# A hybrid decoder layer: the input projection by seven products of blocks, and the mLSTM heads as a stage of their own

## The chip, the cores and the metric

The kernel runs on one core of a Trainium2 chip. The core has a matmul engine (PE, whose weight loads, PEld, overlap its products), three engines for other arithmetic (DVE, ACT and POOL) and SP, which issues the DMAs. The metric is the time of one execution in device microseconds, lower is better. It is in float32, and each matmul operand is cut into a high and a low part of a reduced format, so a product of two matrices is three matmuls: low by high, high by low, and high by high.

## The reference

One decoder layer over 1024 tokens of width 1024. What matters here is its first third:

```python
h = rmsnorm(x, ln1[l])
z = h @ w_in[l]
ml_qk, ml_v, ml_o, ml_i, ml_f, fx_q, fx_k, fx_v, fx_f = jnp.split(z, splits, axis=-1)
ml_qk = jax.nn.silu(causal_conv(ml_qk, ml_conv_w[l], ml_conv_b[l]))
mq, mk = jnp.split(ml_qk.astype(jnp.float32), 2, axis=-1)
...
mh = mlstm_chunkwise(mq, mk, mv, ig, lf)
mh = mh * lax.rsqrt(jnp.mean(mh * mh, axis=-1, keepdims=True) + EPS)
...
ml_out = (mh.reshape(B, S, ML_W) * jax.nn.sigmoid(ml_o)).astype(x.dtype)
fx_out = forgetting_attention(fq, fk, fv, flf).reshape(B, S, FX_W)
x = x + jnp.concatenate([ml_out, fx_out], axis=-1) @ w_out[l]
```

There are four mLSTM heads of width 128 (queries and keys pass a causal convolution of four taps and a silu; an output gate `ml_o`) and eight heads of forgetting attention (fx) of width 64. Then follow cross-attention into 256 memory tokens, a squared-ReLU MLP of width 4096, and a final norm.

## The kernel before

Activations lie with the features on the 128 partitions and the tokens along the free dimension, in two halves of 512 tokens. A tile framework orders each engine's instructions and gives out buffers; program order is the priority, and an instruction whose buffer or operand is not there yet can be overtaken. Some stretches are fixed in order by hand (`in_order`). Working buffers have names and small counts: `act` (seven of 128 x 8 x 512), `w4` (five of 128 x 1024), `z4` (two), `wr` for raw weights (two), `wh` and `wl` for their cut parts (three each), and `r_a` to `r_f`, `r_p`, `r_y` of 128 x 512 (one or two each, from `w2`). PSUM has eight banks (`sc` three, `tp` two, `mm`, `m2` (rows name it m) and `ov` one each).

The parts that matter, in program order:

- Lines 381 to 423: x is cut into the operands `h` (high and low for each half, gain folded in), and the first mLSTM values and the gates are made along the way.
- Lines 676 to 682: the other half of the values (`token_major`, eight units of 24 matmuls with 256 columns), the gate rows, and the memory tokens' preparation. All mLSTM values stay in two `act` buffers, `mv`.
- `ml_project` (L656): for each mLSTM head five output tiles of 128 features: the key, an fx query, the query, an fx key, and the output gate. Each tile is eight blocks of the contraction times three matmuls times two halves, by `proj` (L258). `conv_silu` (L502) follows the keys and queries, `carried` and `carry` make the state that the first half of the tokens hands to the second.
- `ml_head` (L568): for each half of the tokens four blocks: scores on PE, weights `exp` on ACT, a mask on POOL, products on DVE, a cut on ACT and DVE, and the sum with the values in the bank `ov`. Then (after its first `yield`) the closing: the factors go through DRAM (`facd`) to a row, and are multiplied in. The numerators of the two halves lie in the two `r_f` buffers until then.
- Line 683 on: head by head, `ml_head` of one head stands ahead of `ml_project` of the next, whose `next(closing)` calls place the steps of the closing between projections.
- Line 1088 on: 13 leading slots of the attention (scores only), then the fx values (`token_major` with `w_fv`, sixteen units), then the attention slots, in which a filler of key and value units of the cross-attention and of output units runs at a given rate.

`mm3` (L184) records every three-matmul product, so its three lines L186 to L188 gather most of PE's time, and `split` (L131) every cut, with ACT at L134 or L137 and DVE at L135 or L138. A sum of the helper `sub` has line L1339.

## Time and profile before

| what | value |
| --- | --- |
| timed runs, median of 3 | 1512.34 us (1508.72 to 1514.9) |
| span of the profiled execution, first to last instruction | 1509.2 us |
| granted PE clock, mean over that span | 0.997 |
| DMA | 303.04 MB, mean 201 GB/s |
| HBM read and written | 202.75 MB and 98.82 MB |

Of the profiled execution the page gives the span and no other time of its own; the median of the timed runs is 3.1 us above that span, and the lowest of them 0.5 us below it. A line of the groups view gives line, engine, operation, the written tile and those read, shapes, count, busy time, the mean of one in ns, and the engine's idle time ahead of the group with what ended it. The windows view gives busy time of each engine in stretches of the span. PE's busy time is modelled from pipelined matmuls: a matmul shown with 395 ns starts 230 ns after the one before it.

### The profile page before, as it was taken

To read this page: it belongs to the slowest core of one execution; us is meant where nothing else is said; L and a number is where in the kernel's file an instruction comes from. 1 tells how busy PE (TensorE), PEld (TensorE's weight loads), DVE (VectorE), ACT (ScalarE), POOL (GpSimd) and SP (SyncE) were. 2 spreads that over 40 slices of the span, in tenths; PEclk is the share of its full clock that TensorE was granted. 3 is DMA by queue.
4 is the path that set the end of the run, shared out by engine and by line. 5 is a ranking of instruction groups with operands and counts; after the bars stand their busy time and mean duration, and the time that the engine had idled before them with its cause. 6 is when DMAs were issued, how large, how long until landed. Compare 5 with 4: busy or idle time off the path is not lost.

```text
span 1509.2 us, 22358 instructions
## 1 busy us (share of the span) xinstructions
PE 1493.0 (99%) x7806; PEld 1263.7 (84%) x7806; DVE 1122.7 (74%) x1803; ACT 757.7 (50%) x1440; POOL 528.7 (35%) x545
## 2 busy tenths in 40 slices
PE   9999999999999999999999999999999999999997
PEld 9988888889899888788988878888888888888887
DVE  7766676664788875667767899989996678787765
ACT  7324343334688764566654467566664521122134
POOL 1003030414365441623300044454544365553312
PEclk9999999999999999999999999999999999999999
DMA  6322333435777877853354447676678677776623
GB/s 243 115 79 95 98 108 126 132 129 153 247 261 256 284 248 246 271 169 126 128 182 159 147 155 279 235 261 248 217 273 292 264 279 279 279 272 251 247 88 112
DMA packets 124276, 303.04 MB, mean 201 GB/s; under 512 B 13810, under 2 KB 28460, under 8 KB 117252
## 3 DMA queue, kind: packets, MB, share of 16 engines
q1 hardware_dynamic: 124164, 301.62, 57.3%
q8 instruction: 61, 1.00, 0.3%
q14 instruction: 51, 0.42, 0.1%
HBM read 202.75 MB, written 98.82 MB: 200 GB/s over the span
## 4 chain that ended last, share of the span: by engine, by line
PE 90%; DMA 4%; DVE 3%; ACT 1%; issue 1%; POOL 1%; POOLq 0%; DVEq 0%; SPq 0%; ACTq 0%
PE tp L186 8%; PE tp L187 8%; PE tp L188 8%; PE sc L186 6%; PE sc L188 6%; PE sc L187 6%; PE mm L186 5%; PE m L188 5%; PE m L186 5%; PE m L187 5%; PE mm L188 5%; PE mm L187 5%; PE ov L801 2%; PE ov L186 2%; PE ov L187 2%; PE ov L188 2%
## 5 line engine op out<-in xcount | busy, mean ns | idle before, releaser
L186 PE MATMUL tp<-act,wl 128*128 128x512 f32 (+1 forms) x440 | 172.6, 392 | 0.0
L187 PE MATMUL tp<-act,wh 128*128 128x512 f32 (+1 forms) x440 | 172.1, 391 | 0.0
L188 PE MATMUL tp<-act,wh 128*128 128x512 f32 (+1 forms) x440 | 171.8, 392 | 0.0
L135 DVE TENSOR_TENSOR wl<-wr,wh 128x1024 fp32r<-128x1024 f32 (+2 forms) x99 | 131.4, 1327 | 27.0 <-ACT wh L134 26.7
L134 ACT ACTIVATE wh<-wr 128x1024 fp32r<-128x1024 f32 (+2 forms) x99 | 99.8, 1008 | 85.7 <-PE tp L188 32.7
L186 PE MATMUL mm<-act,wl 128*128 128x512 f32 (+1 forms) x332 | 124.8, 376 | 2.6 <-DVE r_c L138 2.1
L188 PE MATMUL mm<-act,wh 128*128 128x512 f32 (+1 forms) x332 | 124.1, 374 | 0.0
L187 PE MATMUL mm<-act,wh 128*128 128x512 f32 (+1 forms) x332 | 123.8, 373 | 0.0
L186 PE MATMUL m<-act,wl 128*128 128x512 f32 (+1 forms) x308 | 113.8, 369 | 0.6 <-DVE wl L135 0.6
L188 PE MATMUL m<-act,wh 128*128 128x512 f32 (+1 forms) x308 | 113.8, 369 | 0.0
L187 PE MATMUL m<-act,wh 128*128 128x512 f32 (+1 forms) x308 | 113.7, 369 | 0.0
L188 PE MATMUL sc<-act,wh 128*128 128x512 f32 (+1 forms) x280 | 105.6, 377 | 0.0
L187 PE MATMUL sc<-act,wh 128*128 128x512 f32 (+1 forms) x280 | 105.6, 377 | 0.0
L186 PE MATMUL sc<-act,wl 128*128 128x512 f32 (+1 forms) x280 | 105.6, 377 | 0.0
L1612 POOL TENSOR_TENSOR z<-wr 128x256 f32<-128x256 f32 x56 | 52.9, 966 | 131.8 <-DMA wr<-w_ff2q 126.7
L188 PEld LDWEIGHTS tp<-act,wh 128*128 128x128 f32 x440 | 82.7, 188 | 19.0
L186 PEld LDWEIGHTS tp<-act,wl 128*128 128x128 f32 x440 | 82.7, 188 | 18.5
L187 PEld LDWEIGHTS tp<-act,wh 128*128 128x128 f32 x440 | 82.7, 188 | 18.2
L134 ACT ACTIVATE wh<-z 128x1024 fp32r<-128x1024 f32 (+1 forms) x54 | 55.5, 1027 | 81.8 <-POOL z L1612 62.3
L135 DVE TENSOR_TENSOR wl<-z,wh 128x1024 fp32r<-128x1024 f32 (+1 forms) x54 | 77.7, 1439 | 11.4 <-ACT wh L134 11.4
L134 ACT ACTIVATE w<-wr 128x768 fp32r<-128x768 f32 (+3 forms) x35 | 28.0, 801 | 107.4 <-PE tp L186 33.0
L186 PEld LDWEIGHTS mm<-act,wl 128*128 128x128 f32 x332 | 62.7, 189 | 14.2 <-DVE r_c L138 2.6
(734 smaller groups left out, 4387.2 us busy)
## 6 DMA issues: line engine op xcount, KB each, us to landing
act<-right SPq DMA_DIRECT2D x49, 1024.0 KB
right<-w SPq DMA_DIRECT2D x56, 256.0 KB
wr<-w_ff2q SPq DMA_DIRECT2D x28, 512.0 KB
right<-r_d SPq DMA_DIRECT2D x49, 256.0 KB
right<-r_e SPq DMA_DIRECT2D x49, 256.0 KB
act<-fqk SPq DMA_DIRECT2D x48, 256.0 KB
wr<-w_in SPq DMA_DIRECT2D x20, 512.0 KB
wr<-w_ff SPq DMA_DIRECT2D x20, 512.0 KB
```

The lines of the kernel that those rows point to most:

```text
L134: s.activation(hi, src, AF.Copy)
L135: return v.tensor_tensor(out=lo, in0=src, in1=hi.bitcast(F32), op=ALU.subtract)
L186: nc.tensor.matmul(ps, w[1], x[0], start=first, stop=False, skip_group_check=more)
L187: nc.tensor.matmul(ps, w[0], x[1], start=False, stop=False, skip_group_check=more)
L188: nc.tensor.matmul(ps, w[0], x[0], start=False, stop=last, skip_group_check=more)
L801: nc.tensor.matmul(self.ov[:, c0:], self.fv[:, self.j], t[:, c0:], start=self.j == 0 and t is self.p[1], stop=self.last and t is self.p[0])
L1612: g.tensor_tensor(out=o, in0=x, in1=y, op=op)
```

## The change

The 20 tiles of the input projection are taken as ten pairs of two tiles (two for the gates, then for each head a pair of key and query and a pair of fx query and key). For a pair, the weights are a 2 x 2 arrangement of blocks (two tiles by two halves of the contraction) and h another (two halves of the contraction by two halves of the tokens), and the product is made by seven products of blocks with sums before and after, instead of eight. The sums of h's blocks (t1 to t4) are made by `in_right`, which loads x again; the sums of the weights by `left_in`; the sums after by `InPair.run`. Keys and queries (`kqd`), gates (`ogd`) and mLSTM values (`mvd`) are stored to DRAM. The heads then form a stage of their own, which loads them back (`ml_loads`), with four units of the fx values placed around each head. In the head's loop `carry` stands ahead of the closing of the head before. Half of the key and value units of the cross-attention are taken out of the attention slots and put behind the 13 leading slots, and the filler's rate goes from 4.6 to 3.5.

The diff, cut to its core:

```diff
-    mv = (act(), act())
+    mvd = dram.tile([MLH, P, 8, 2 * P], F32, name="mvd")
     def mv_sink(t, c, ps):
-        o = mv[c][:, t].rearrange("p (h e c) -> p h e c", h=2, e=2)
+        o = rotate("b", "p", "c").bitcast(F32R).rearrange("p (h e c) -> p h e c", h=2, e=2)
         split(o[:, :, 0], o[:, :, 1], ps.rearrange("p (h c) -> p h c", h=2), rcol[:, t : t + 1])
+        load(mvd[2 * c : 2 * c + 2, :, t].rearrange("h p c -> p h c"), o.bitcast(F32).rearrange("p h e c -> p h (e c)"))
...
-    def conv_silu(n, hi, lo):
-        w = weights(a["w_in"][n])
-        z = z4()
-        g.memset(z[:, 0:3], 0.0)
-        for _, hf, ps in proj(w, h, 1):
-            v.tensor_tensor(out=z[:, 3 + hf * TH : 3 + hf * TH + TH], in0=ps, in1=row[:, hf * TH : hf * TH + TH], op=ALU.mult)
-        y = z4()[:, :T]
+    def conv_silu(z, which, hd):
+        n = MLH * which + hd
+        y = w4()
         cw = VEC["conv_w"] + 4 * n
-        v.tensor_scalar(out=y, in0=z[:, 0:T], ...)
+        s.activation(y, z[:, 0:T], AF.Identity, scale=vec[:, cw : cw + 1], bias=...)
         for j in range(1, 4):
             v.scalar_tensor_tensor(out=y, in0=z[:, j : j + T], scalar=vec[:, cw + j : cw + j + 1], in1=y, op0=ALU.mult, op1=ALU.add)
         t = z[:, 0:T]
         s.activation(t, y, AF.Tanh, scale=0.5)
         v.scalar_tensor_tensor(out=y, in0=t, scalar=1.0, in1=y, op0=ALU.add, op1=ALU.mult)
-        split(hi, lo, y, 0.5)
-        return y
+        split(t.bitcast(F32R), y.bitcast(F32R), y, 0.5)
+        load(kqd[hd, which, 0], t)
+        load(kqd[hd, which, 1], y)
+    def whole(parts, hf):
+        t = w2("p")
+        c = slice(hf * TH, hf * TH + TH)
+        g.tensor_tensor(out=t, in0=parts[0][:, c].bitcast(F32), in1=parts[1][:, c].bitcast(F32), op=ALU.add)
+        return t
...
-    def fx_project(which, n):
...
-    def ml_project(hd):
...
+    I_RIGHT = {}
+    for c, hf, k0 in (("11", 0, 0), ("21", 0, 4), ("22", 1, 4)):
+        I_RIGHT[c] = [both(h[hf], lambda t: t[:, k0 + k]) for k in range(4)]
+    for c in ("t1", "t2", "t3"):
+        t = act()
+        I_RIGHT[c] = [(t[:, k], t[:, 4 + k]) for k in range(4)]
+    I_RIGHT["t4"] = [(t[:, :TH], t[:, TH:]) for t in (w4(dt=F32R) for _ in range(4))]
+    def in_right(k):
+        x = {}
+        for c, tag, hf, n in (("11", "d", 0, k), ("12", "e", 1, k), ("22", "f", 1, 4 + k), ("21", "p", 0, 4 + k)):
+            x[c] = w2(tag)
+            load(x[c], a["x"][:, n, hf * TH : hf * TH + TH])
+            s.activation(x[c], x[c], AF.Copy, scale=vec[:, VEC["ln1"] + n :][:, 0:1])
+        y = x["11"]
+        sub(y, x["12"], y)
+        split(*I_RIGHT["t1"][k], y)
+        sub(y, x["22"], y, g)
+        split(*I_RIGHT["t2"][k], y)
+        sub(x["12"], x["22"], x["12"], g)
+        split(*I_RIGHT["t3"][k], x["12"])
+        sub(y, x["21"], y, g)
+        split(*I_RIGHT["t4"][k], y)
+    for k in range(4):
+        in_right(k)
+    I_NAMES = {1: "11", 2: "21", 5: "t1", 6: "t2", 3: "22", 7: "t3", 4: "t4"}
+    i_cycle = ("sc", "mm", "tp", "sc", "m2", "tp", "sc", "ov")
...
+    in_pairs = [("o", 0), ("o", 1)]
+    for hd in range(MLH):
+        in_pairs += [("kq", hd), ("fx", hd)]
...
+    in_both = lambda p_: [(q_, i) for i in I_NAMES for q_ in (p_, p_ + 1)]
+    in_jobs = in_both(0)
+    for p_ in range(2, IP):
+        in_jobs += [(p_, 1)] + ([(p_ - 1, 4)] if p_ > 2 else []) + [(p_, i) for i in (5, 2, 6, 3, 7)]
+    in_jobs.append((IP - 1, 4))
...
+    def left_in(p_, group):
+        if group == 0:
+            in_raws[p_] = [sb("wr", [P, 1024], 2) if p_ != 1 else z4()[:, :1024] for _ in range(2)]
+            for raw, n in zip(in_raws[p_], reversed(in_tiles(*in_pairs[p_]))):
+                load(raw, a["w_in"][n])
+        r2, r1 = in_raws[p_]
+        x11, x12, x21, x22 = r1[:, :TH], r1[:, TH:], r2[:, :TH], r2[:, TH:]
+        if group == 0:
+            h22, l22 = (w2(t, dt=F32R) for t in "bc")
+            split(h22, l22, x22)
...
+        hi, lo = (sb(t, [P, 1024], 3, F32R) for t in ("wh", "wl"))
+        split(hi, lo, (r1, r2, r1)[group])
+        if group == 0:
+            by = g if p_ > 1 else v
+            by.tensor_tensor(out=x21, in0=x21, in1=x22, op=ALU.add)
+            sub(x22, x21, x11, by)
+            sub(x12, x12, x22, by)
+            sub(x11, h22.bitcast(F32), x22, by)
+            by.tensor_tensor(out=x11, in0=x11, in1=l22.bitcast(F32), op=ALU.add)
...
+    class InPair:
...
+        def run(self, i, l):
+            r = I_RIGHT[I_NAMES[i]]
+            at_ = {1: "a", 2: "a", 5: "c", 3: "c", 6: "b", 7: "b", 4: "b"}[i]
+            if i in (1, 5, 6):
+                setattr(self, at_, i_bank())
+            ps = getattr(self, at_)
+            for k in range(4):
+                mm3(ps, both(l, lambda t: t[:, k]), r[k], i in (1, 5, 6) and k == 0, k == 3, True)
+            u = self.u
+            if i == 1:
+                self.p1 = w2("p") if self.kind != "o" else firsts[:, TH * self.i :][:, :TH]
+                s.activation(self.p1, ps, AF.Copy)
+            elif i == 2:
+                v.tensor_tensor(out=self.room("11", "a", "y"), in0=ps, in1=self.row_of("11"), op=ALU.mult)
+                self.done("11")
+            elif i == 5:
+                self.add(self.room("22", "e"), ps, self.p1)
...
+        def scale(self, c):
+            g.tensor_tensor(out=self.u[c], in0=self.u[c], in1=self.row_of(c), op=ALU.mult)
+            self.done(c)
+        def done(self, c):
+            n, hf = int(c[0]) - 1, int(c[1]) - 1
+            x, at_ = self.u[c], slice(hf * TH, hf * TH + TH)
+            if self.kind == "o":
+                s.activation(x, x, AF.Tanh, scale=0.5)
+                load(ogd[2 * self.i + n, :, at_], x)
+            elif self.kind == "fx":
+                hi, lo = w2("d", dt=F32R), x.bitcast(F32R)
+                split(hi, lo, x, None if n else FXD ** -0.5)
+                load(fqk[n, 0, self.i, :, at_], hi.bitcast(F32))
+                load(fqk[n, 1, self.i, :, at_], x)
+            elif c in ("12", "21"):
+                conv_silu(self.z[n], 1 - n, self.i)
+    firsts = w4()
+    for at, (p_, i) in enumerate(in_jobs):
+        while in_prep and in_first[in_prep[0]] <= at + 5:
+            left_in(*in_prep.pop(0))
...
+        pair.run(i, in_cuts.pop((p_, i)))
...
+    def ml_loads(hd):
+        qk = quarters(F32R)
+        for t, src in zip(qk, (kqd[hd, 1, 0], kqd[hd, 1, 1], kqd[hd, 0, 0], kqd[hd, 0, 1])):
+            load(t.bitcast(F32), src)
+        mv = [w4((P, 4, 256), F32R) for _ in range(2)]
+        for i, t in enumerate(mv):
+            load(t.bitcast(F32), mvd[hd, :, 4 * i : 4 * i + 4])
+        og = w4()
+        load(og, ogd[hd])
+        return qk[2:], qk[:2], lambda j: mv[j // 4][:, j % 4], og
...
     for hd in range(MLH):
-        closing = ml_head(hd, *ready)
+        q, k, values, og = ml_loads(hd)
+        weighed = weigh(hd)
+        state = carried(hd, whole(k, 0), values, *weighed)
+        sums = carry(hd, q, whole(q, 1), *state)
+        next(closing, None)
+        fv_next(1)
+        next(closing, None)
+        fv_next(1)
+        closing_now = ml_head(hd, q, k, values, og, *sums)
+        next(closing, None)
+        closing = closing_now
         next(closing)
-        if hd < MLH - 1:
-            ready = ml_project(hd + 1)
+        fv_next(2)
+    fv_next(16)
...
-    units = []
+    units, early = [], []
     for n in range(XH):
+        if n == 2:
+            early, units = units, []
         units += [key_unit(2 * n), value_unit(n), key_unit(2 * n + 1)]
...
-    token_major(a["w_fv"], fv_sink, between={4: lambda: next(closing, None)})
     hm = act().rearrange("p a b -> p (a b)").rearrange("p (e k c) -> p e k c", e=2, k=KT)
     load(hm.bitcast(F32), hmd)
+    for i, (srcs, run) in enumerate(early):
+        if i == 3:
+            next(closing, None)
+        for step in run([weights(src) for src in srcs]):
+            f = step[2] if step[1] else None
+            while f:
+                f = f()
...
-    RATE, DELAY = 4.6, 3
+    RATE, DELAY = 3.5, 3
```

More of the change, by code (lines that the diff above doesn't have):

```diff
@@ L540, in carried @@
             for t in (kl, kh):
-                nc.tensor.matmul(ps[:, 0:256], t[:, j * P : (j + 1) * P], mv_of(hd, j), start=j == 0 and t is kl, stop=j == 3 and t is kh)
+                nc.tensor.matmul(ps[:, 0:256], t[:, j * P : (j + 1) * P], values(j), start=j == 0 and t is kl, stop=j == 3 and t is kh)
         c32 = w2("c", P)
@@ new lines, in hybrid_layer @@
+    in_both = lambda p_: [(q_, i) for i in I_NAMES for q_ in (p_, p_ + 1)]
[3 more added lines that the diff above has]
+    in_jobs.append((IP - 1, 4))
+    I_GROUP = {1: 0, 2: 0, 5: 1, 6: 1, 7: 2, 3: 2}
+    in_first = {}
+    for at, (p_, i) in enumerate(in_jobs):
+        if i in I_GROUP:
+            in_first.setdefault((p_, I_GROUP[i]), at)
+    in_prep = sorted(in_first, key=in_first.get)
@@ new lines, in hybrid_layer, with fv_next @@
+    banks[:] = ["mm", "tp", "m2", "tp"]
+    fv_steps = [t for c in range(2) for t in [token_units(a["w_fv"], fv_sink, c)]]
+    def fv_next(n):
+        while n and fv_steps:
+            try:
+                next(fv_steps[0])
+                n -= 1
+            except StopIteration:
+                fv_steps.pop(0)
+    for hd in range(MLH):
[10 more added lines that the diff above has]
+        closing = closing_now
```

130 lines of the change are left out of this document (76 added, 54 removed).

## The prediction

> **What bounds the kernel now.** I read the page first: the busy table, then the chain that ended last.
>
> ```profile
> span 1509.2 us, 22358 instructions
> ...
> PE 1493.0 (99%) x7806; PEld 1263.7 (84%) x7806; DVE 1122.7 (74%) x1803; ACT 757.7 (50%) x1440; POOL 528.7 (35%) x545
> ...
> PE 90%; DMA 4%; DVE 3%; ACT 1%; issue 1%; POOL 1%; POOLq 0%; DVEq 0%; SPq 0%; ACTq 0%
> ```
>
> The matmul engine (PE) is busy all the time and carries 90% of the chain. As a busy PE need not be a full PE, I next took the windows view, cut where the work around the change begins and ends. Its columns are length, then busy time and instruction count of PE, weight load, DVE, ACT and POOL, then the granted clock, the DMA share and GB/s.
>
> ```profile
> 61.40:331.20 269.80, 269.80 (x1291) 223.31 (x1290) 178.24 (x271) 97.39 (x158) 50.88 (x63) 1.00 0.34 109
> 331.20:393.00 61.80, 60.39 (x486) 59.00 (x485) 34.81 (x86) 27.97 (x68) 22.50 (x28) 1.00 0.58 182
> 393.00:590.00 197.00, 196.01 (x1253) 174.67 (x1252) 158.01 (x413) 145.01 (x397) 97.02 (x149) 1.00 0.76 257
> ...
> 900.00:1000.00 100.00, 100.00 (x430) 80.38 (x429) 90.50 (x101) 67.00 (x107) 47.06 (x30) 1.00 0.74 261
> ```
>
> The rows are the input projection with the mLSTM heads among it; the forgetting values (fv) with the 13 leading slots; the attention slots; and a stretch of the MLP's first product, which already uses seven products. That last row holds only 512-column matmuls and gives a rate: 100/430 = 0.2326 us each. The groups view of 61.4 to 331 by shape counts the same kind here (each row stands for three, L186 to L188, with equal counts):
>
> ```profile
> L186 PE MATMUL tp<-act,wl 128*128 128x512 f32 x160 | 63.6, 398 | 0.0
> ...
> L186 PE MATMUL mm<-act,wl 128*128 128x512 f32 x80 | 31.8, 398 | 0.0
> ...
> L186 PE MATMUL m<-act,wl 128*128 128x512 f32 x80 | 31.6, 395 | 0.0
> ```
>
> 3 x (160 + 80 + 80) = 960 = 20 tiles x 2 halves x 8 x 3. At 0.2326 that is 223.3 of the 269.8 us; 331 small matmuls of the heads share the other 46.5, with no idle time ahead of any group. So the stage is bound by matmul count.
>
> **The change part by part.**
>
> *Seven products.* Ten pairs x 7 products x 4 blocks x 3 = 840 matmuls of 512 columns in place of 960. 120 x 0.2326 = **-27.9 us**. This is arithmetic in the code, so "it doesn't do what it says" is no case here.
>
> *The start.* Blocks t1 to t4 have to be made from x, read a second time, and the first two pairs' weights summed on DVE. What can this hide behind?
>
> ```profile
> 40.00:61.00 21.00, 21.00 (x181) 20.41 (x181) 16.55 (x42) 10.59 (x23) 1.01 (x1) 1.00 0.31 104
> 61.00:69.00 8.00, 8.00 (x46) 6.38 (x45) 8.00 (x9) 2.44 (x4) 0.00 (x0) 1.00 0.45 119
> 69.00:76.00 7.00, 7.00 (x35) 5.85 (x35) 0.61 (x5) 0.81 (x2) 0.69 (x1) 1.00 0.49 112
> ```
>
> ```profile
> L135 DVE TENSOR_TENSOR wl<-wr,wh 128x1024 fp32r<-128x1024 f32 x21 | 25.5, 1215 | 0.2
> ...
> L507 DVE TENSOR_TENSOR z<-tp,row 128x512 f32<-128x512 f32 x8 | 5.5, 687 | 10.8 <-PE tp L188 10.8
> ```
>
> A 512-wide DVE operation costs 0.69 us, a 1024-wide cut 1.22. The first four jobs (11.2 us of PE, 12 matmuls each) need only slices of h. The fifth, at about 72.6, needs t1 (4 x 2 x 0.69 = 5.5), the first pair's cuts and sums (2 x 1.22 + 6 x 0.69 = 6.6), the second pair's first cut (1.2) and an eviction (0.7): 14.0 us of DVE. From 61.4 DVE has 11.2 us, less some 5 us of gate work that stays, plus 4.4 us idle before 61: about 10.6, so 3.4 us late. The sixth job waits for the second pair's rest, 5.4 us of DVE in 2.8 us: 2.6 more. ACT has room (2.44 of 8, 0.81 of 7). The x loads stand on SP's queue ahead of the weights, and their rooms d, e, f, p hold two blocks only, so the third and fourth wait for the first two. Idle PE has a second price, seen where the cross-attention queries start:
>
> ```profile
> 640.00:650.00 10.00, 8.26 (x37) 6.94 (x38) 5.64 (x8) 5.00 (x9) 2.25 (x3) 0.83 0.83 306
> ```
>
> ```profile
> PE mm L186 <- DVE r_c L138: 2.1, 1, 2.1
> ```
>
> ```profile
> 643.23 0.43 PE mm L187
> ...
> 648.22 0.23 PE mm L188
> ```
>
> The window's clock is 0.83: after a wait of 2.1 us for DVE, pieces of the chain take 0.43 us in place of 0.23 for some 4 us, about 2 us more. The Trainium skill ("TensorE: Matmul & The Clock Gate", What's actually happening) speaks against a change that opens gaps: after an idle window of about 3.4 us the clock halves until PE has been busy as long, an estimated 1.7 us beyond the gap by that page's figures. The trace agrees, though its gap was 2.1 us. Here 3.4 + 2.6, with the dip partly under it: **+7 us**. Ends: 0, as the MLP's first product starts at full rate in the before trace (the 870 to 900 us window runs 134 matmuls in 30.00 us), and 15, if DVE takes all four blocks (20 x 0.69 = 13.8) ahead of the weights.
>
> ```profile
> 870.00:900.00 30.00, 30.00 (x134) 24.38 (x133) 27.84 (x38) 17.61 (x28) 13.18 (x8) 1.00 0.43 142
> ```
>
> *The pairs.* A key/query pair and an fx pair take 168 x 0.2326 = 39.1 us of PE. DVE in that time: 6 weight cuts of 1024 and 2 of 512 (8.7), 12 evictions (8.2), 4 fx cuts (2.8), two convolutions of 3 taps, a gate product and a cut:
>
> ```profile
> L512 DVE SCALAR_TENSOR_TENSOR z<-z,vec,z 128x1024 f32<-128x1024 f32 x24 | 31.6, 1318 | 0.2
> ...
> L515 DVE SCALAR_TENSOR_TENSOR z<-z,z 128x1024 f32<-128x1024 f32 x8 | 9.7, 1216 | 1.2 <-ACT z L514 1.2
> ```
>
> ```profile
> L135 DVE TENSOR_TENSOR wl<-wr,wh 128x1024 fp32r<-128x1024 f32 x8 | 14.0, 1747 | 0.6 <-ACT wh L134 0.6
> ```
>
> ```profile
> L1339 POOL TENSOR_TENSOR wr<-wr,wr 128x512 f32<-128x512 f32 x6 | 8.8, 1466 | 24.7 <-DVE r_c L135 12.6 <-DVE wl L135 7.7 <-issue 4.4
> ```
>
> 2 x (3 x 1.32 + 2 x 1.22) = 12.8, in all 32.5 of 39.1. But POOL now sums beside it (5 weight sums and 3 scalings a pair), and in 900 to 1000, where POOL does such sums (last two rows), the same cut takes 1.747, not 1.215. If the 24.3 us that read two SBUF operands all grew by 1.44, DVE would need 43.2: 4.1 us over, x 4 = 16 us. Against that, the MLP's pairs, so slowed, left PE at full rate with DVE at 90.5. The stage also moves 18 MB more (x again 4, values 4, keys and queries 8, gates 2), in 196 us some 92 GB/s above the 109 of the first window, below the 261 of the last. Between 0 and 16 I take the value near that row: **+3 us**. The Trainium skill names the cause ("GPSIMD Engine Reference", Specifications: SBUF interfaces shared with VectorE, contended by instructions with two SBUF inputs). By that rule, with every such instruction overlapped, the term would be the 16 of the rows; it is a rival below.
>
> *The heads.* Their bodies keep their matmuls, but projections no longer fill around them, only fv does: 384 matmuls of 256 columns at half of 0.2326 = 44.7 us, 16 units, four a head. The fourth body, in the second window, is about a quarter of 46.5, 11.6. PE has 46.5 + 11.6 + 44.7 = 103 us of work here, then 28 us in the lead-in: the early key and value units (192 x 0.116 = 22.3) and the scores (61.8 - 44.7 - 11.6 = 5.5). Together 131, or 32.7 us a head. Is a head slower than that by its own chain?
>
> ```profile
> L603 ACT ACTIVATE r_f<-ov x4: 598/598/599, 136.0 to 342.1; 128x512 f32<-128x512 f32 x4
> ```
>
> ```profile
> L617 DVE TENSOR_TENSOR c_fac<-c_fac,c_rd x4: 166/168/169, 165.1 to 369.0; 128x8 f32<-128x8 f32 x4
> ```
>
> ```profile
> L628 DVE SCALAR_TENSOR_TENSOR r_f<-r_f,vec,r_a x8: 750/752/753, 177.6 to 383.6; 128x512 f32<-128x512 f32 x8
> ```
>
> ```profile
> 371.60 1.94 DMA facd<-r_a
> 373.56 5.12 DMA r_a<-facd
> ...
> 379.49 4.05 DMA r_a<-facd
> ```
>
> First and last starts give a head's second half: 165.1 - 136.0 = 29.1 (first head), 369.0 - 342.1 = 26.9 (last). The first closing product starts 177.6 - 165.1 = 12.5 later, most of it the DMAs in the last rows. `carry` now stands ahead of the closing that frees its buffer f, and the half-head's numerator takes the other f: behind it wait the copy out of the one `ov` bank, and the next half's matmuls. So a period holds a closing and a second half. At the measured lengths (12.5, some 5 of products, cut and store, 27) that is 45. But the 27 was spent among projections or fv with higher or equal claim; the instructions of a block by themselves (ACT 0.7, POOL 0.4, DVE 0.7, ACT 0.6, DVE 0.7, PE 0.7) add to 3.8 us and two buffers overlap, so four blocks with the sums and factors can be 17: 16 + 17 = 33. Each head also reads 7 x 0.5 MB back; four make 14 MB, at the 182 to 261 GB/s of the windows above 54 to 77 us beside 131, so not the bound. I take 33: 0.3 us a head over, and one dip with the first load: **+4 us**, between 0 and 4 x (45 - 32.7) = 49.
>
> *The slots.* Half of the key and value units leave them: 22.3 us of PE go, counted above in the lead-in, where fv's 44.7 had gone to the heads. DVE had 158.0 and ACT 145.0 of 197; about 11 us of DVE leave too (evictions and half cuts at 0.4 to 0.7), so DVE rises from 80% to 147/174.7 = 84%. **+2 us** for slots that wait on it; 0 if they never do, 22 if the slots have a pace of their own, which 196.01 us of PE in 197 speaks against.
>
> *Sum.* -27.9 + 7 + 3 + 4 + 2 = -11.9. The span of 1509.2 would be 1497.3. The timed runs' median, 1512.34, lies 3.1 above this span; with that kept, 1500.4.
>
> **The rivals.**
> *All hidden* (no added term costs anything): 1512.3 - 27.9 = 1484. For it: the dense start at 870. Against: DVE full from 61 to 69.
> *DVE sets the pairs' pace* (16 in place of 3): -11.9 + 13 = +1, 1513. For it: 1.747 against 1.215. Against: the 430 matmuls in 100 us with DVE at 90.5. It decides where DVE's need passes 39.1 us a double pair, a slowing of 1.27.
> *The heads' chain sets the pace*: the place is the wait for f behind the closing's DMAs, the price up to 49 in place of 4, -11.9 + 45 = +33, 1545. It decides at 32.7 us a head; the total turns slower than before from 32.7 + 16/4 = 36.7. For it: the first and the last head both took over 26 us for a half. Against: fv of later heads, early units and scores may run in such gaps.
>
> **How the numbers follow.** About 0.5% (7.6 us) can be told from no change. Forecast 0.60 (its own range 1490 to 1508; 0.50 of it faster, 0.10 within), all hidden 0.08, DVE's pace 0.15 (0.12 within, 0.03 slower), the heads 0.17 (0.02 within, 0.15 slower). Faster 0.58, same 0.24, slower 0.18. The range begins at the full gain, 1484, and ends at 1518, past DVE's case and into the weaker half of the heads'; what lies above is under 2 in 10.
>
> **What would show it.** 840 matmuls of 512 columns in the pairs at 0.233 us; if 430 a 100 us is missed there with DVE near 100, the pairs' term is wrong. PE idle, and a clock below 1.00, around 70 to 90: the start. L617's successor starting every 33 us with PE dense: the heads' term; 36 us or more, or PE idle between heads, makes the prediction wrong on the other side. The slots' stretch shorter by about 20 us.

## The result, and the profile after

The changed kernel takes 1678.42 us (median of 4 runs, 1675.88 to 1681.24), the kernel before 1510.71 us (median of 4 runs beside them): 1.111 times as long, 95% interval 1.108 to 1.113. It is slower by 168 us, far above the range that was given.

The page of the changed kernel, the lines that answer to those of before:

```profile
span 1679.5 us, 22595 instructions
...
PE 1537.1 (92%) x7686; PEld 1285.5 (77%) x7686; DVE 1220.5 (73%) x1861; ACT 810.7 (48%) x1502; POOL 662.3 (39%) x627
...
PE 45%; DVE 3%; ACT 1%; DMA 1%; issue 1%; POOL 0%; POOLq 0%; DVEq 0%; ACTq 0%
```

The matmuls are 7686, 120 fewer, as counted. The shares of the chain add to 51% only: it could be followed back no further than 807.9 us, which is later than all that the change touches, so its 45% for PE can't be set beside the 90% of before. But the clock row of the page has 5 to 7 tenths in two places. The windows view, cut by the stages (length, then PE, weight load, DVE, ACT and POOL, the clock, the DMA share, GB/s):

```profile
61.40:147.70 86.30, 57.08 (x211) 41.10 (x209) 53.80 (x71) 37.45 (x59) 33.55 (x22) 0.74 0.32 102
147.70:301.90 154.20, 139.01 (x567) 109.06 (x568) 127.64 (x112) 58.39 (x69) 99.37 (x63) 0.97 0.38 135
301.90:365.60 63.70, 47.89 (x264) 41.77 (x263) 37.74 (x46) 21.45 (x31) 18.12 (x18) 0.87 0.76 272
365.60:542.70 177.10, 120.39 (x604) 108.30 (x603) 79.26 (x166) 58.43 (x122) 58.18 (x70) 0.68 0.41 127
542.70:583.30 40.60, 34.24 (x227) 30.58 (x228) 24.62 (x56) 19.18 (x44) 8.05 (x11) 0.87 0.74 229
583.30:765.00 181.70, 180.53 (x1084) 156.48 (x1083) 146.55 (x393) 133.94 (x370) 84.60 (x141) 1.00 0.74 247
```

A busy PE at half clock is not much work: from each matmul's columns at 0.2326 us per 512, the work in the first five rows is 42, 132, 42, 63 and 28 us, against 86, 154, 64, 177 and 41 us of time. The loss is at the start (first row: two pairs with the sums of h's blocks), a little in the pairs (second), and above all from the last pair to the end of the heads (third to fifth). The slots (last row) are 15 us shorter than before (393 to 590 us there), as forecast to within 5 us.

Three rows place the stages. The copy of a pair's first product is L779 here; `w` is the copy of the first pair, and of the `r_p` rows the three from bank `sc` hold the third pair's (first start) and the tenth's (last start). L621 ends a head's factors, as L617 did:

```profile
L779 ACT ACTIVATE r_p<-sc x3: 578/599/600, 147.7 to 301.9; 128x512 f32<-128x512 f32 x3
...
L779 ACT ACTIVATE w<-tp x1: 578/578/578, 113.4 to 113.4; 128x512 f32<-128x512 f32 x1
```

```profile
L621 DVE TENSOR_TENSOR c_fac<-c_fac,c_rd x4: 155/163/167, 385.4 to 542.7; 128x8 f32<-128x8 f32 x4
```

So the third pair starts about 2.8 us before 147.7, where 61.4 + 39.1 + 7 was forecast (first copy 110.3); a pair takes (301.9 - 147.7) / 7 = 22.0 us in place of 19.55; and a head (542.7 - 385.4) / 3 = 52.4 us, where 33 was forecast and 36 named as the point from which it is slower.

### The profile page after: what moved, and what is told of

Read it like the earlier page. It is cut to its first block, busy times and chain, and to the rows that moved or that the text cites. A ratio compares the mean times of both kernels' runs of the same rounds, so it can differ in the third digit from the quotient of the medians.

```text
span 1679.5 us, 22595 instructions
## 1 busy us (share of the span) xinstructions
PE 1537.1 (92%) x7686; PEld 1285.5 (77%) x7686; DVE 1220.5 (73%) x1861; ACT 810.7 (48%) x1502; POOL 662.3 (39%) x627
## 4 chain that ended last, share of the span: by engine, by line
PE 45%; DVE 3%; ACT 1%; DMA 1%; issue 1%; POOL 0%; POOLq 0%; DVEq 0%; ACTq 0%
PE sc L189 5%; PE sc L190 5%; PE sc L191 5%; PE tp L189 3%; PE tp L191 3%; PE tp L190 3%; PE m L190 2%; PE m L189 2%; PE m L191 2%; PE mm L191 2%; PE mm L189 2%; PE mm L190 2%; PE ov L189 2%; PE ov L191 2%; PE ov L190 2%
## 5 line engine op out<-in xcount | busy, mean ns | idle before, releaser
L135 DVE TENSOR_TENSOR wl<-wr,wh 128x1024 fp32r<-128x1024 f32 (+2 forms) x114 | 159.0, 1396 | 48.5 <-ACT wh L134 48.4
L189 PE MATMUL sc<-act,wl 128*128 128x512 f32 (+1 forms) x384 | 146.8, 383 | 7.1 <-DVE wl L135 6.2
L190 PE MATMUL sc<-act,wh 128*128 128x512 f32 (+1 forms) x384 | 146.2, 381 | 0.0
L191 PE MATMUL sc<-act,wh 128*128 128x512 f32 (+1 forms) x384 | 145.9, 381 | 0.0
L189 PE MATMUL tp<-act,wl 128*128 128x512 f32 (+1 forms) x300 | 118.2, 394 | 11.2 <-DVE wl L135 7.1
L190 PE MATMUL tp<-act,wh 128*128 128x512 f32 (+1 forms) x300 | 117.2, 391 | 0.0
L191 PE MATMUL tp<-act,wh 128*128 128x512 f32 (+1 forms) x300 | 117.0, 390 | 0.0
L189 PE MATMUL mm<-act,wl 128*128 128x512 f32 (+1 forms) x272 | 102.9, 378 | 6.5 <-ACT act L134 5.0
L190 PE MATMUL mm<-act,wh 128*128 128x512 f32 (+1 forms) x272 | 103.1, 379 | 1.0 <-DVE act L135 1.0
L191 PE MATMUL mm<-act,wh 128*128 128x512 f32 (+1 forms) x272 | 102.9, 378 | 0.0
L141 POOL TENSOR_TENSOR wr<-wr,wr 128x512 f32<-128x512 f32 x38 | 55.5, 1461 | 97.0 <-DVE r_c L135 30.8
L135 DVE TENSOR_TENSOR wl<-z,wh 128x1024 fp32r<-128x1024 f32 (+1 forms) x57 | 82.3, 1443 | 15.5 <-ACT wh L134 15.5
L189 PEld LDWEIGHTS sc<-act,wl 128*128 128x128 f32 x384 | 72.7, 189 | 24.6 <-DVE wl L135 8.1
L190 PEld LDWEIGHTS sc<-act,wh 128*128 128x128 f32 x384 | 72.8, 190 | 15.0
L191 PEld LDWEIGHTS sc<-act,wh 128*128 128x128 f32 x384 | 72.4, 189 | 15.3
```

Source lines behind the costliest of these rows:

```text
L135: return v.tensor_tensor(out=lo, in0=src, in1=hi.bitcast(F32), op=ALU.subtract)
L141: by.tensor_tensor(out=out_, in0=x, in1=y, op=ALU.subtract)
L189: nc.tensor.matmul(ps, w[1], x[0], start=first, stop=False, skip_group_check=more)
L190: nc.tensor.matmul(ps, w[0], x[1], start=False, stop=False, skip_group_check=more)
L191: nc.tensor.matmul(ps, w[0], x[0], start=False, stop=last, skip_group_check=more)
```

## The experiments

Each kernel is one run beside the kernel before on the same chip (1510.6 to 1512.9 us there). The changed kernel's four runs lie 5.4 us apart, so a single run that differs from it by less shows nothing. "Period" is the time from one head's factors to the next, by the row of that line (the expectations count it between the numerators' copies, which gives 0.5 us more in the changed kernel and up to 4.4 in others). In the six kernels below that keep the heads and change only the start or the pairs, it lies between 49.9 and 52.6 us, so a change of period by 2 or 3 us shows nothing either.

### What the heads cost in each kernel

Two kernels leave the heads' arithmetic out.

```diff
-        weighed = weigh(hd)
-        state = carried(hd, whole(k, 0), values, *weighed)
-        sums = carry(hd, q, whole(q, 1), *state)
...
-        closing_now = ml_head(hd, q, k, values, og, *sums)
+        closing_now = ml_none(hd, og)
```

> The changed kernel without the mLSTM heads: weigh, carried, carry and ml_head are left out, the gate row goes to mix in place of the closing's products; projections, loads and fv stay. Theory 'the heads' chain sets the pace': it saves the heads' 58 us of matmuls and 90 to 120 us in which PE waited, to 1500 to 1530 us. Rival 'the loads, fv and the early units are slow there by themselves': it saves 58 to 75 us, to 1603 to 1620 us.

> The kernel before with the same left out. Theory 'the projections cover the heads' chain': it saves their 58 us of matmuls and no more than 12 us besides, to 1440 to 1455 us. Rival 'the heads cost waits there as well': it saves over 80 us, below 1430 us.

Measured: 1531.84 us, near what the theory of the chain said, and 1467.78 us, outside both theories. The same heads cost 1678.4 - 1531.8 = **147 us** after the change and 1511.0 - 1467.8 = **43 us** before it, less than their 58 us of matmuls by my estimate. In the kernel before, up to the first product of attention weights and values, it is 55 us (342.7 in place of 397.6 us); the stretch behind the slots is 12 us longer in that run, and why was not looked into. By this point of the span the heads cost 146 us after the change (439.5 in place of 585.9). So 91 to 103 of the 168 us are the heads without their cover. The other 64 to 76 us (1531.8 against 1467.8, and these 12) lie in the start, the pairs and the way from the pairs to the slots, and are so although 28 us of products went. This way in the changed kernel without heads:

```profile
331.00:440.00 109.00, 77.44 (x571) 72.42 (x569) 43.18 (x89) 33.87 (x74) 20.93 (x23) 0.84 0.95 332
```

It takes 109 us for 68 us of matmuls by their columns, at a DMA share of 0.95, so hiding the heads' chain would not by itself make it dense. That the loads set its time was not tried.

### The start

In the changed kernel, PE's waits from 61.4 to 147.7 us (waiter, what it waited for, us in total, times, longest), and a few of the loads that SP issued:

```profile
PE ov L237 <- DVE r_b L229: 6.6, 1, 6.6
PE ov L189 <- ACT act L134: 5.7, 1, 5.7
PE mm L189 <- ACT act L134: 5.0, 2, 3.5
```

```profile
66.59 0.33 SPq L675 DMA_DIRECT2D r_f<-x  x1
...
76.39 0.42 SPq L305 DMA_DIRECT2D hmd<-r_e  x1
...
91.41 0.33 SPq L675 DMA_DIRECT2D r_e<-x  x1
...
101.02 0.33 SPq L675 DMA_DIRECT2D r_d<-x  x1
```

L675 reads x for the blocks; L305 stores the memory tokens' parts, out of the same buffers d, e, f and p. Two loads of the first block go out at 18 us, the other fourteen from 66.6 us on among these stores, the last at 101.0. Four kernels move this work.

```diff
 # memory tokens later
-    with tc.issue_after(last_sum.ins):
-        mem_prepare()
...
     for k in range(4):
         in_right(k)
+    with tc.issue_after(last_sum.ins):
+        mem_prepare()
```

> The memory tokens' preparation is placed behind in_right in program order; nothing is left out. Theory 'rooms' (the blocks' x loads wait until the preparation's stores free r_d, r_e, r_f, r_p): the x loads go out before 60 us, PE is dense some 30 to 45 us earlier than at 114, about 1640 us. Rival 'the blocks' own chain' (cut on ACT, sums on DVE and POOL, one block after the other): under 10 us gained, about 1672.

```diff
 # jobs first (and, in the next kernel, mem_prepare() behind all pairs)
-    for k in range(4):
-        in_right(k)
...
     for at, (p_, i) in enumerate(in_jobs):
+        if at == 4:
+            for k in range(4):
+                in_right(k)
```

> in_right stands behind the first four jobs in program order (the memory tokens' preparation where the change has it); nothing is left out. Theory 'order' (ACT takes its work in a fixed order, and the copy of the first product stands behind the cuts of t1 to t4, which wait for x): the first copies come before 80 us in place of 113, the third pair's begins 20 to 25 us earlier, about 1655 us. Rival 'the blocks' chain' (the blocks themselves are late, by their rooms and DVE's work): the fifth job is no earlier, under 8 us gained.

> in_right behind the first four jobs, and the memory tokens' preparation behind all the pairs; nothing is left out. Theory 'two causes' (rooms held by the preparation, and the first copies behind the cuts on ACT, each worth some 10 us, add): the third pair's first copy, at 147.7 us in the changed kernel, comes at about 122, about 1655 us. Rival 'the blocks' own work sets the floor' (DVE is full with gates, cuts and sums): at 135 or later, over 1665 us.

```diff
 # as the last, from the high parts of h
-            load(x[c], a["x"][:, n, hf * TH : hf * TH + TH])
-            s.activation(x[c], x[c], AF.Copy, scale=vec[:, VEC["ln1"] + n :][:, 0:1])
...
+        x11, x12, x22, x21 = (h[hf][0][:, n].bitcast(F32) for hf, n in ((0, k), (1, k), (1, 4 + k), (0, 4 + k)))
```

> As the run with in_right behind four jobs and the memory tokens' preparation behind the pairs, where the third pair's first copy came at 123.0 us; besides, t1 to t4 are made from the high parts of h and x is not loaded again (left out: the low parts in these sums, 16 loads and 16 scalings). Theory 'the second load of x': the third pair's first copy comes at 108 to 113 us. Rival 'DVE's and POOL's sums and cuts among the gates' work': at 118 or later.

Measured: 1672.12, 1668.96, 1677.34 and 1672.22 us. With the memory tokens later, six x loads went out by 19 us and the last by 80, and PE still waited:

```profile
PE tp L189 <- ACT w L778: 19.0, 1, 19.0
```

The first product was done by 68 us, and its copy on ACT, at 98.0, stood behind the cuts of t3 and t4 and, by then, the memory tokens' squares and cuts. The third pair's copy came at 140.6. With the jobs first, with both, and with both and no second load of x, the third pair's copy is the first start of these rows:

```profile
L776 ACT ACTIVATE r_p<-sc x3: 572/597/601, 136.9 to 290.6; 128x512 f32<-128x512 f32 x3
```

```profile
L773 ACT ACTIVATE r_p<-sc x3: 572/597/598, 123.0 to 274.0; 128x512 f32<-128x512 f32 x3
```

```profile
L769 ACT ACTIVATE r_p<-sc x3: 578/597/600, 125.7 to 276.4; 128x512 f32<-128x512 f32 x3
```

From 147.7 us to 140.6 with the memory tokens later, 136.9 with the jobs first, 123.0 with both, 125.7 without the second load: rooms and order together are worth 25 us, and the second load of x nothing. What is left, 123 against 103 without any loss, lies beside a DVE that the last of these kernels shows nearly full; it was not taken apart further:

```profile
60.00:80.00 20.00, 16.30 (x102) 13.77 (x102) 17.38 (x17) 9.83 (x17) 10.68 (x4) 0.86 0.28 81
80.00:100.00 20.00, 16.04 (x62) 12.05 (x61) 19.83 (x24) 9.39 (x15) 10.59 (x6) 0.84 0.19 57
```

Little of the 25 us reached the end. The tenth pair's copy came at 274.0 in place of 301.9 us, the first head's numerator at 352.4 in place of 365.6, its factors at 380.0 in place of 385.4, and the time, 1 us less, can't be told from the changed kernel's. The memory tokens' preparation now lies at the end of the pairs and ahead of the heads, from 279 us on; that it alone takes the gain back was not tried.

### The pairs

```diff
 # weight sums on DVE
-            by = g if p_ > 1 else v
+            by = v
```

> The five weight sums of each of the eight later pairs go from POOL to DVE. Theory 'weight chain' (load, cut, five POOL sums of 1.46 us in a row, next cuts, in one set of raw buffers, holds PE up): the pairs' stage is 15 to 25 us shorter, about 1658 us. Rival 'DVE is the bound of the pairs': 40 more sums of about 0.7 us, 10 to 28 us longer, about 1697.

```diff
 # looking eight jobs ahead
-        while in_prep and in_first[in_prep[0]] <= at + 5:
+        while in_prep and in_first[in_prep[0]] <= at + 8:
```

> The changed kernel with the weights of a pair prepared eight jobs ahead in place of five; nothing else. Theory 'late cuts' (the raw weights' only two buffers come free with the third cut, which is placed five jobs ahead): a pair's pitch falls from 22.0 to under 21 us, 5 to 12 us gained. Rival 'the three buffers of the cuts hold it': within 4 us of the changed kernel.

Measured: 1669.10 us (pitch of a pair 21.0) and 1675.81 us (22.2). Placing the cuts earlier does nothing, as the rival said. Putting 40 more sums on DVE makes it faster, and the groups view of the same seven pairs shows why; first the changed kernel, then this one:

```profile
L135 DVE TENSOR_TENSOR wl<-wr,wh 128x1024 fp32r<-128x1024 f32 x22 | 34.6, 1574 | 8.2 <-ACT wh L134 8.2
L510 DVE SCALAR_TENSOR_TENSOR w<-z,vec,w 128x1024 f32<-128x1024 f32 x18 | 33.8, 1880 | 7.5 <-ACT w L508 7.4
```

```profile
L135 DVE TENSOR_TENSOR wl<-wr,wh 128x1024 fp32r<-128x1024 f32 x22 | 31.2, 1422 | 4.7 <-ACT wh L134 4.7
L510 DVE SCALAR_TENSOR_TENSOR w<-z,vec,w 128x1024 f32<-128x1024 f32 x18 | 23.4, 1298 | 0.0
L141 DVE TENSOR_TENSOR wr<-wr,wr 128x512 f32<-128x512 f32 x14 | 9.5, 681 | 0.1
```

```profile
147.30:294.10 146.80, 135.74 (x553) 107.27 (x554) 129.54 (x146) 56.91 (x67) 34.31 (x25) 0.96 0.40 141
```

and POOL's sums in the changed kernel:

```profile
L141 POOL TENSOR_TENSOR wr<-wr,wr 128x512 f32<-128x512 f32 x16 | 25.2, 1577 | 7.1 <-DMA wr<-w_in 2.8 <-DVE wl L135 2.4 <-DVE r_c L135 0.7
L141 POOL TENSOR_TENSOR wr<-r_b,wr 128x512 f32<-128x512 f32 x8 | 17.7, 2212 | 0.0
```

A tap of the convolution (L510) takes 1.88 us while POOL sums beside it and 1.30 when POOL does not; the cut 1.57 and 1.42. DVE does 146 instructions in 129.5 us of busy time, where it did 112 in 127.6: the slowing by POOL's sums had cost DVE nearly what it now spends on them itself, and on POOL they took 1.6 to 2.2 us each, where DVE takes 0.7 (wr<-wr,wr). That is the rule that the prediction cited from the Trainium skill ("GPSIMD Engine Reference", Specifications), and here the trace agrees with it, for the tap in the size that I had put aside (1.45) and for the cut in a smaller one (1.11). Of the 17 us that seven pairs lose, 7 went with POOL's sums. Neither theory had it right, one expecting 15 to 25, the other a loss; whether the shorter way of the weights or the faster DVE gives the 7 was not separated. In the other 10 PE waits for weight cuts (L135) with DVE 88% busy, and no run here takes these away.

### The heads: which wait

The end of one head in the changed kernel, on DVE (start, duration, line, operation; in brackets the idle time and what ended it):

```profile
483.84 0.69 DVE L603 TENSOR_TENSOR r_f<-ov,r_f 128x512 f32<-128x512 f32 x1 [0.60 <-PE ov L191]
...
489.00 0.16 DVE L613 COPY c_sqs<-sc 128x4 f32<-128x4 f32 x1 [2.87 <-ACT c_dens L612]
...
490.10 0.17 DVE L201 TENSOR_SCALAR c_var<-c_sqs 128x8 f32<-128x8 f32 x1
492.79 0.75 DVE L566 SCALAR_TENSOR_TENSOR r_b<-r_p,c_m,r_c 128x512 f32<-128x512 f32 x1 [2.53 <-ACT r_c L561]
493.46 0.16 DVE L209 TENSOR_TENSOR c_t<-c_y 128x8 f32<-128x8 f32 x1
...
496.43 0.48 DVE L138 SCALAR_TENSOR_TENSOR r_p<-m,rcol,r_p 128x256 fp32r<-128x256 f32 x1 [2.41 <-ACT r_p L137]
496.83 0.16 DVE L621 TENSOR_TENSOR c_fac<-c_fac,c_rd 128x8 f32<-128x8 f32 x1
...
504.39 0.75 DVE L632 SCALAR_TENSOR_TENSOR r_f<-r_f,vec,r_a 128x512 f32<-128x512 f32 x1 [4.64 <-DMA r_a<-facd]
```

From the numerator (483.8) to the closing's product (504.4) DVE works 5 us and waits the rest: for ACT, behind ACT for PE's sums, for POOL's root (1.65 us, done at 492.0) and a product of the next head that stands ahead (492.8), for an fv cut that stands ahead in its fixed order (496.4), and for the factors' way through DRAM (4.64). Eight kernels take suspected waits away, one or two at a time.

```diff
 # closing first
         weighed = weigh(hd)
+        next(closing, None)
+        fv_next(1)
+        next(closing, None)
         state = carried(hd, whole(k, 0), values, *weighed)
+        next(closing, None)
```

```diff
 # fb in z4
-            fb = w2("a")
+            fb = z4()[:, :TH]
```

```diff
 # rooms: eight slices of an act buffer for nmb, fb and the numerators
-            fb = w2("a")
+            fb = ml_rooms(4 + hf)
...
-        num, den = w2("f"), w2("b")
+        num, den = ml_rooms(2 + hd % 2), w2("b")
```

> In the loop over heads the closing of the head before stands ahead of carried and carry, as it did before the change. Theory 'order' (carry ahead of the closing is what makes the period long): period per head from 52 to about 36 us, about 1620 us. Rival 'rooms' (the closing's rows and the next head's rows share the one r_a buffer, whatever the order): within 10 us of 1678.

> The closing's rows fb lie in the two z4 buffers, which are idle in this stage, in place of the one r_a buffer; order as in the changed kernel. Theory 'r_a' (the next head's row nmb waits for the closing): a head's first half runs beside the closing of the head before, period from 52 to about 38 us, 40 to 60 us gained, about 1628 us. Rival 'r_f or the blocks' own chain': period stays over 48 us, at most 12 us gained.

> In the heads' stage the rows nmb and fb and the numerators lie in eight slices of an act buffer of their own, in place of r_a (one) and r_f (two); order as in the changed kernel. Theory 'rooms' (a head waits for the closing of the one before): period per head from 53 to 36 to 40 us, 45 to 60 us gained, about 1625 us. Rival 'the half's own chain' (27 us from the copy of the first half's numerator to the factors, as measured in both kernels, plus the first half): period 45 us or more, at most 32 us gained, over 1646 us.

```diff
 # fv first
     for k in range(4):
         in_right(k)
+    for c in range(2):
+        for _ in token_units(a["w_fv"], fv_sink, c):
+            pass
...
 # fv first, wt in eight slices of an act buffer
-                wt = acc if j == 0 else w2("c")
+                wt = acc if j == 0 else ml_wt(hd % 2 * 4 + j % 4)
```

> The sixteen fv units stand behind in_right and ahead of the pairs, none are left among the heads. Theory 'the heads are bound by their chain': 44.7 us of matmuls fill PE's hole at the start and leave a stage that PE does not bound, so the period per head stays over 45 us, and the time falls by 15 us at most (1663 to 1678 us). Rival 'the heads are bound by PE at half clock': the period falls by 8 us or more a head, 1640 us or less.

> The kernel with fv first, and the heads' weights wt in eight slices of an act buffer (free there, since h is no longer read) in place of the two r_c buffers; nothing else. Theory 'r_c' (a head's eight blocks, its squares, e and c32 pass through two buffers, each held through ACT, POOL, DVE and POOL again): the period falls from 45 us to 36 or less, 25 us or more gained, under 1653 us. Rival 'the chain's own steps and the fixed orders of the engines': over 42 us, at most 12 us gained.

```diff
 # two heads in flight (ml_head yields after each block)
+    for at in range(AT * MLH + 12):
+        for hd in range(MLH):
+            if at >= AT * hd:
+                next(steps_[hd], None)
...
-            num = ov_()
+            num = ps_tile(("ov", "m2")[hd % 2])
...
 # and the cuts of wt in slices of their own
-                wh, wl = w2("d", dt=F32R), w2("e", dt=F32R)
+                wh, wl = ml_cut(hd % 2 * 4 + j % 2 * 2), ml_cut(hd % 2 * 4 + j % 2 * 2 + 1)
```

> Two heads are in flight: program order takes their blocks in turn, the next head begins when the one before is at its second half; rows and numerators lie in an act buffer of their own, sums of weights in r_b and r_f in turn, numerators' banks are ov and m2 in turn, gates in z4; fv units stay among them. Theory 'one head's chain of small operations sets the pace': the period falls from 53 to about 30 us, about 1605 us. Rival 'engines and queues that all heads share set it': over 42 us, over 1640 us.

> The last two kernels together, and the weight sums on DVE as in an earlier run. Theory 'one head's chain': with two chains in flight PE's work counts again, so fv's 44.7 us, moved into the hole at the start, are gained where they gained nothing by themselves: 35 to 45 us below the run with two heads alone, about 8 more from the weight sums, about 1560 us. Rival: at most 15 us below the run with two heads alone.

> The kernel with fv first, two heads in flight and the weight sums on DVE, and besides wt in eight and its cuts wh and wl in eight slices of act buffers, so that two heads share none of these. Theory 'scratch rooms' (two heads could not overlap because they shared r_c, r_d and r_e): the period falls from 38 to about 25 us, 35 to 50 us gained, about 1605 us. Rival 'the fixed orders of the engines': over 34 us, at most 15 us gained.

Measured, by the factors' rows:

| kernel | factors, first to last head | period | time |
| --- | --- | --- | --- |
| changed | 385.4 to 542.7 | 52.4 | 1678.42 |
| closing first | 392.7 to 545.8 | 51.0 | 1683.57 |
| fb in z4 | 385.2 to 525.7 | 46.8 | 1664.99 |
| rooms for rows and numerators | 384.5 to 516.2 | 43.9 | 1653.80 |
| fv first | 410.7 to 541.1 | 43.5 | 1677.86 |
| fv first, rooms for wt | 403.6 to 522.2 | 39.5 | 1658.89 |
| two heads in flight | 395.7 to 514.9 | 39.7 | 1656.03 |
| fv first, two heads, sums on DVE | 406.5 to 506.9 | 33.5 | 1647.91 |
| the last, rooms for wt and its cuts | 394.6 to 474.7 | 26.7 | 1612.97 |

Three of the rows themselves, of rooms, of fv first and of the last kernel:

```profile
L621 DVE TENSOR_TENSOR c_fac<-c_fac,c_rd x4: 159/167/926, 384.5 to 516.2; 128x8 f32<-128x8 f32 x4
```

```profile
L621 DVE TENSOR_TENSOR c_fac<-c_fac,c_rd x4: 155/161/168, 410.7 to 541.1; 128x8 f32<-128x8 f32 x4
```

```profile
L623 DVE TENSOR_TENSOR c_fac<-c_fac,c_rd x4: 150/166/168, 394.6 to 474.7; 128x8 f32<-128x8 f32 x4
```

What follows, in turn, each from one run. **Order** is no cause: with the closing first the time is no lower. **The wait for r_a and r_f behind the closing**, the mechanism of my rival, is real and small in the changed kernel: 5.6 us a head for the row, 8.5 with the numerators. **fv among the heads** costs 8.9 us a head; its cuts pass through the heads' buffers b, c and p and stand in the engines' fixed orders, but which of the two it is was not taken apart. That gain was given back: the 44.7 us of matmuls delay the pairs by 15 us (third pair at 162.9), and the first factors come 25 us later; where the other 10 us go was not looked into. The time stood still, as the theory of the chain said; the period fell to 45.3 by the count of the expectations, just over its bound. **Buffers of their own for wt**, with one head at a time, give 4.0 us a head and 19 us of time, between the two theories. **Two heads in flight** help little (39.7, or 33.5 with fv first, 8 us of time where 35 to 45 were expected) while both pass through r_c, r_d and r_e, and give 26.7 and 35 us with buffers of their own, as the theory of the scratch buffers expected. So these are what kept two chains from running beside each other; which of them did was not taken apart.

Did a head itself get shorter? Its second half with the factors lies between the copy of the first half's numerator and the factors' row. In the changed kernel's second head that is 29 us:

```profile
413.35 0.60 ACT L607 ACTIVATE r_f<-ov 128x512 f32<-128x512 f32 x1 [1.35 <-PE ov L191]
...
442.28 0.15 DVE L621 TENSOR_TENSOR c_fac<-c_fac,c_rd 128x8 f32<-128x8 f32 x1
```

In the four heads it is 19.8, 28.9, 28.7 and 18.3 us, with fv first 23.6 to 18.2, with buffers for wt besides 13.4 to 17.0, and in the last kernel 16.7 to 22.1. So this part did get shorter. What stays with one head at a time is the other part, from the factors to the next head's copied numerator: 26 to 28 us in the changed kernel and still 24 to 25 in the one with buffers for wt. There the next head's row waits for the one r_a buffer behind the closing again:

```profile
403.57 0.17 DVE L621 TENSOR_TENSOR c_fac<-c_fac,c_rd 128x8 f32<-128x8 f32 x1
...
413.91 0.32 SPq L579 DMA_DIRECT2D r_a<-rows  x1
...
417.36 0.72 ACT L590 ACTIVATE r_b<-r_a,gcol 128x512 f32<-128x512 f32 x1 [2.03 <-DMA r_a<-rows]
...
427.30 0.57 ACT L607 ACTIVATE r_f<-ov 128x512 f32<-128x512 f32 x1
```

The first half itself takes 10 us here, and 14 lie ahead of it. One head at a time with both, buffers for wt and for the rows, was not tried.

What is left in the last kernel is cover:

```profile
310.00:370.00 60.00, 42.34 (x162) 33.56 (x161) 40.98 (x49) 23.52 (x36) 22.22 (x22) 0.76 0.83 299
370.00:470.00 100.00, 76.88 (x334) 66.10 (x333) 66.35 (x134) 42.79 (x94) 58.48 (x64) 0.67 0.47 164
```

In the 102 us from the first head's copied numerator (372.9) to the last factors PE has 31 us of work by its columns, and in the 42 us ahead of them, which begin with the end of the last pair, 13. That leaves (102 - 31) + (42 - 13) = 100 us without work. The kernel's span is 102 us longer than the kernel before's with 28 us of products fewer, 130 us in all; so some three quarters of what it lacks lie here. In the stretch ahead of the heads the DMA share is 0.83 as well (first row).

Last, whether the halved clock is a cause:

```diff
 # behind each block's product with the values
+                for _ in range(8):
+                    nc.tensor.matmul(warm, q[0][:, 0:P], q[0][:, 0:TH], start=True, stop=True)
```

> The changed kernel with eight matmuls of 512 columns into an unused bank behind each block's product with the values: 256 more, 60 us at 0.23 us each, in a stage where PE waits for over 100 us. Theory 'half clock' (the granted clock, 0.68 in the heads, doubles the matmuls that lie on a head's chain): the clock rises over 0.85, the period falls from 53 by 4 us or more a head, 12 to 40 us gained. Rival 'the chain is of the other engines, and matmuls that stand in PE's fixed order delay it': the period grows, 0 to 60 us lost.

Measured: 1680.87 us.

```profile
365.00:545.00 180.00, 140.14 (x800) 124.79 (x799) 80.22 (x173) 59.84 (x126) 58.89 (x71) 0.85 0.40 127
```

```profile
L624 DVE TENSOR_TENSOR c_fac<-c_fac,c_rd x4: 166/170/852, 396.7 to 542.2; 128x8 f32<-128x8 f32 x4
```

The clock rose from 0.68 to 0.85, and the last factors came at 542.2 in place of 542.7 us (the first head 11 us later, the period 48.5). So a higher clock bought in this way gains nothing. What the low clock costs by itself is not separated: the added matmuls stand in PE's order ahead of the heads' own, and fv's units have one bank less here, so a faster PE and a longer queue may have cancelled. The Trainium skill ("TensorE: Matmul & The Clock Gate", HAM oscillation) warns of such gaps as a cost of PE, and the granted clock of 0.68 agrees; but filling them gained nothing in this stage.

## Why the prediction was wrong

The forecast was a span of 1497.3; the profiled one is 1679.5, 182 us more. The sum, term by term:

| term | forecast | measured | from |
| --- | --- | --- | --- |
| seven products | -27.9 | -27.9 | 7806 - 7686 matmuls at 0.2326 |
| the start | +7 (0 to 15) | +44 | third pair's copy 147.7 - 61.4 - 39.1 - 2.8 |
| the pairs | +3 (0 to 16) | +17 | 7 x (22.03 - 19.55), seven of the eight pairs |
| the heads, with the way in and out | +4 (0 to 49) | about +129 | what the other terms leave of 170.3, the two spans' difference |
| the slots | +2 (0 to 22) | about +7 | 181.7 in place of 197 - 22.3 |

*Seven products.* Right, and shown by the count.

*The start.* The step that failed is "The x loads stand on SP's queue ahead of the weights, and their rooms d, e, f, p hold two blocks only". It counted the blocks against each other and not against the memory tokens' preparation, which holds the same four rooms ahead of them; I had listed that preparation in the kernel and not asked when it lets go. Nor did I ask where ACT's copy of the first product stands. The runs show 25 us of the 44 for these two, none for the load of x. The other 20 us lie beside DVE's full time, which I did count, with 3.4 + 2.6; that DVE makes all of them is not shown.

*The pairs.* The mechanism was named and the size wrong: between 0 and 16 I chose the value by a stretch of the MLP in which a slowed DVE did not hold PE. The rival "DVE sets the pairs' pace" had the size, 16, and its slowing is there (1.88 against 1.30 for a tap, a factor 1.45; the rival had 1.44). That DVE alone set the pace is not shown, since it was 83% busy in these pairs (127.6 of 154.2).

*The heads.* The step that failed is "so four blocks with the sums and factors can be 17: 16 + 17 = 33". The first starts of L607 (copied numerator of the first half) are 365.6, 413.3, 468.1 and 524.3, those of L621 385.4, 442.3, 496.8 and 542.7. So the 17 was 20 in the first head and 18 in the last, but 29 in the two between, which share engines and buffers with fv and with the next head's loads and sums (13 to 17 where fv stood elsewhere and wt had buffers); and the 16 (its own parts, 12.5 and some 5, add to more), from the factors to the next head's copied numerator, was 26 to 28, since the next first half followed the closing in place of running beside it. A sum of instructions gave the length of a half that is alone, and the two in the middle are not. The rival "the heads' chain" named the right place and, with 45 a head, was nearer, but it too missed two things: fv, taken for filling, lengthens the chain by 9 us a head; and the way into the first head, priced at "one dip", is 36 us from the end of the pairs' last product (about 330) to the copied numerator at 365.6, as the loads of its values go out only at 331.6 and 335.4 us, when that product has read t4 out of the buffers they need. Of the 182 us some 125 are this term; leaving the heads out of both kernels puts 91 to 103 on them alone.

*The slots* came out as forecast to 5 us.

Whether the kernel could carry the heads among the pairs, as before, was not tried: t1 to t4 and h fill the seven `act` and four of the five `w4` buffers there. The 10 us that remain in the pairs, and what the heads would need to be covered, stay open.

## What to carry to other kernels

A chain of small operations that other work has covered can cost its measured length when that work goes away (45 us a head by the rows of before, 52 measured), not the sum of its instructions (33): leave it out of the kernel before moving it, and see what it costs there. When a change gives a buffer a new user, look up in the trace of before who holds that buffer at that time, and what stands ahead of the new work in each engine's fixed order. A mended wait counts only where the next stage is not late for another reason, so follow a gain to the end of the span before believing it.

## What the runs showed of the hardware

POOL's two-input sums slow DVE beside them far more than I had expected: 1.88 against 1.30 us for a 1024-wide multiply-add on DVE. And a 512-wide sum that took POOL 1.6 to 2.2 us takes DVE 0.7 to 0.8. The granted clock stood at 0.68 over the 177 us of the heads, and PE is shown busy for 120 us over 63 us of work: its share of busy time says little until the clock beside it is read. In such a stretch both PE (36% of the time at full rate) and the DMA (a share of 0.41, 127 GB/s) are low, which the Trainium skill ("Perfetto Trace Analysis", Roofline) reads as bound by waits and dependencies; the runs agree.
